# Attention gates ahead of the delta gates, query buffers taken by two blocks, one power for three row blocks

## The chip, the cores and the metric

The kernel runs on one core of a Trainium2 chip. The metric is device time in microseconds (us) of one execution. A core has a matrix engine (TensorE, PE in the rows; PEld is its loading of the stationary operand), a vector engine (VectorE, DVE), an engine for activation functions and copies (ScalarE, ACT), a general engine (GpSimd, POOL) and one that issues DMAs (SyncE, SP). Each takes its instructions in the order of the program and waits at an instruction until what it depends on is done. Results of TensorE land in PSUM, which is shared out here as two buffers for each of the names `tp`, `pj`, `sc` and `rc`.

## The reference

Two layers on 2048 prompt tokens and 8 samples of 16 tokens each, 1024 wide. Layer 0 mixes a sliding-window attention (branch A, 8 query heads) with a gated delta rule (branch B, 4 heads), each times its own SiLU gate; layer 1 is a pooling layer.

```python
def ab_layer(h, norm_g, w_in, ...):
    z = rms_norm(h, norm_g) @ w_in
    a_q, a_k, a_v, a_g, b_qkv, b_g, b_beta, b_alpha = split_cols(z, AB_WIDTHS)
    q = rms_norm(a_q.reshape(Bn, T, A_HEADS, A_HEAD_DIM), q_norm)
...
    o_a = o_a.reshape(Bn, T, A_WIDTH) * jax.nn.silu(a_g)
    c, new_hist = causal_conv(b_qkv, conv_hist, conv_w)
    bq, bk, bv = jnp.split(c, 3, axis=-1)
...
    o_b, s_new = gated_delta_rule(bq, bk, bv, beta, g, s0.astype(f32), chunk)
    o_b = rms_norm(o_b, o_norm).astype(h.dtype).reshape(Bn, T, B_WIDTH) * jax.nn.silu(b_g)
    y = h + jnp.concatenate([o_a, o_b], axis=-1) @ w_out
```

Inside the delta rule a unit lower triangular system is solved for each block of tokens (`triangular_solve`).

## The kernel before

**Groups and weights.** The tokens are worked in four groups of four blocks of 128 tokens; group 0 has the sample as a fifth block. Each group runs both layers. A matrix product is made of three products of split operands (a high and a low part each), so most products come in threes: L702 to L704 (weights move, 320 or 512 token columns), L1305 to L1307 (tokens stationary, 256 weight columns). `weight_plan` lists the weights' pieces in the order in which the code asks for them. In group 0 a piece is loaded, split by ScalarE (L471), VectorE and GpSimd (L475) and stored; later groups load the split form.

**Layer 0.** The heads are worked in two pairs. For a pair come keys, queries and values of branch B with their convolution (L885 to L901), the queries of branch A (`a_queries`), and in the background the inverse of the triangular system (`b_inverse`: 31 substitution steps on VectorE, L1019 and L1020; a transposing copy L1024; two stores to DRAM, L1026 and L1027; reloads in another shape, L1035 and L1037; products L1046 and on), the recurrence over the blocks (L1172 to L1220; for the sample L1233 to L1266, then L1272 and the scaling L1277), and the attention (`a_attend`, L1469 to L1500). Then come the gate columns of pair 0 (`gates_early(0)`) with `b_gated` (L1287 transposes the delta rule's result into `tp`, L1289 multiplies it) and `a_gated` (L1294, one VectorE product without a transpose), those of pair 1, and the output product (L735 to L737).

**The queries of branch A.** For each block the product lands in `pj`; ScalarE copies it to a buffer `zs` (L1400; the sample's L1397), the squares' sums go over ScalarE (L1319), VectorE (L1320, L1324) and a GpSimd power (L501), GpSimd multiplies (L1328, L1329). Deferred by `DEF`, `qcols` transposes the four heads' columns into `tp` (L1412); ScalarE (L1414) and VectorE (L1416) scale them into `qs` and so free `tp`.

**What sets the order.** Python code writes the program by a clock of its own: `tick` lets deferred steps (`defer`) and background jobs (`start`) go when their time has come. Large SBUF tiles are taken by hand from 11 big and 6 small buffers (`slot`, `drop`); if none is free, `slot` calls `progress()`, which writes the next deferred step or a job's next step at once. The names in the rows show the kind: `A` is a small buffer, `B` a big one.

**The start.** Blocks 0 and 1 are normalised by columns (`norm_input`), blocks 2 to 4 by `first_rows`: per block half the squares on ScalarE (L526) and half on VectorE (L528), a power on GpSimd (L501), the normalising product on VectorE (L545), then the transposes (L557), ScalarE's L560 and VectorE's L561.

## Time and profile before

| what | us |
|---|---|
| median of 3 runs | 1901.49 (1900.74 to 1903.12) |
| the profiled execution, its time | 1898.98 |
| its span in the trace | 1897.2 |
| TensorE busy in the span | 1824.5 |
| VectorE, ScalarE, GpSimd busy | 1196.4, 733.8, 498.8 |

The span runs from the first to the last instruction of the trace; the execution's own time is 1.8 us longer. Positions below are us from the span's start. Busy TensorE means that a product was under way; a row's idle time is what the engine stood before that instruction, with the instruction that released it.

### The profile page before, as it was taken

The page shows a single profiled execution, that of the slowest core. Times are in us where ns is not written, and L with a number is a line of the kernel's source. Part 1 is how long each engine was busy: PE and PEld are TensorE (multiplying, and loading weights), DVE is VectorE, ACT ScalarE, POOL GpSimd, SP SyncE. Part 2 cuts the span into 40 slices and gives each one's busy share as a digit, 9 for nine tenths or more (in the row PEclk, how much of TensorE's full clock was granted, in tenths as well). Part 3 has the DMA queues.
Part 4 walks back from the last instruction along what each step waited for, and adds up shares of the span by engine and source line. Part 5 has one row for each costly group of instructions (what it writes and reads, how often), then busy time and mean ns, then how long its engine had stood idle before and what let it go on. Part 6 is the DMA issues. An engine that isn't in the chain of part 4 may idle for free.

```text
span 1897.2 us, 30999 instructions
## 1 busy us (share of the span) xinstructions
PE 1824.5 (96%) x11434; PEld 1598.7 (84%) x11434; DVE 1196.4 (63%) x3184; ACT 733.8 (39%) x1883; POOL 498.8 (26%) x628
## 2 busy tenths in 40 slices
PE   6999989999999999999999999999999999999999
PEld 6888888889998888888888988888888988788887
DVE  6797967545664697764445597774345597764342
ACT  4465436323332474262222374261222474261210
POOL 5632451323332522310112413220012413220100
PEclk9998999999999999999999999999999999999999
DMA  7433362756668533435457533435467533435554
GB/s 277 144 133 125 120 226 76 250 195 208 229 234 293 214 119 105 167 118 189 171 204 282 208 115 108 166 130 188 161 217 278 204 117 118 148 134 189 182 189 186
DMA packets 94579, 337.52 MB, mean 178 GB/s; under 512 B 35884, under 2 KB 44332, under 8 KB 64988
## 3 DMA queue, kind: packets, MB, share of 16 engines
q1 hardware_dynamic: 94428, 335.54, 50.8%
q8 instruction: 90, 1.47, 0.3%
q14 instruction: 61, 0.50, 0.1%
HBM read 256.93 MB, written 78.58 MB: 177 GB/s over the span
## 4 chain that ended last, share of the span: by engine, by line
PE 74%; DVE 16%; POOL 3%; issue 3%; ACT 2%; DMA 2%; SPq 0%; DVEq 0%; POOLq 0%; ACTq 0%
PE pj L702 12%; PE pj L704 12%; PE pj L703 12%; PE pj L737 3%; PE pj L735 3%; PE pj L736 3%; PE rc L737 2%; PE rc L735 2%; PE rc L736 2%; DVE tm L1019 2%; DVE A L1020 2%; PE pj L1305 2%; PE pj L1306 2%; PE pj L1307 2%; PE tp L557 1%
## 5 line engine op out<-in xcount | busy, mean ns | idle before, releaser
L702 PE MATMUL pj<-XH,w 128*128 128x512 f32 (+3 forms) x1512 | 546.9, 362 | 5.5 <-ACT cb L876 3.4
L704 PE MATMUL pj<-XH,w 128*128 128x512 f32 (+3 forms) x1512 | 536.2, 355 | 0.0
L703 PE MATMUL pj<-XL,w 128*128 128x512 f32 (+3 forms) x1512 | 535.1, 354 | 0.0
L702 PEld LDWEIGHTS pj<-XH,w 128*128 128x128 f32 x1512 | 288.2, 191 | 33.7 <-ACT cb L876 3.7
L704 PEld LDWEIGHTS pj<-XH,w 128*128 128x128 f32 x1512 | 287.5, 190 | 29.3 <-issue 0.2
L703 PEld LDWEIGHTS pj<-XL,w 128*128 128x128 f32 x1512 | 288.0, 190 | 26.5 <-issue 0.2
L475 POOL TENSOR_TENSOR w<-wst,w 128x640 fp32r<-128x640 f32 (+2 forms) x60 | 105.2, 1754 | 179.0 <-ACT w L471 154.5
L1305 PE MATMUL pj<-w,XH 128*128 128x256 f32 (+1 forms) x368 | 106.8, 291 | 0.3 <-DVE VL L1351 0.3
L1307 PE MATMUL pj<-w,XL 128*128 128x256 f32 (+1 forms) x368 | 104.4, 284 | 0.0
L1306 PE MATMUL pj<-w,XH 128*128 128x256 f32 (+1 forms) x368 | 104.3, 283 | 0.0
L742 DVE TENSOR_TENSOR A<-pj,A 128x512 f32<-128x512 f32 x37 | 25.5, 689 | 101.4 <-PE pj L737 101.4
L737 PE MATMUL pj<-w,B 128*128 128x512 f32 x224 | 87.5, 391 | 0.0
L737 PE MATMUL rc<-w,B 128*128 128x512 f32 x212 | 82.6, 390 | 0.0
L471 ACT CAST w<-wst 128x1024 fp32r<-128x1024 f32 (+1 forms) x60 | 61.2, 1021 | 53.5 <-PE sc L737 42.0
L1723 DVE TENSOR_TENSOR B<-cb 128x526 f32<-128x526 f32 x32 | 24.1, 752 | 75.8 <-ACT cb L1775 75.7
L475 DVE TENSOR_TENSOR w<-wst,w 128x384 fp32r<-128x384 f32 (+2 forms) x60 | 48.1, 804 | 37.3 <-ACT w L471 37.1
L715 DVE SCALAR_TENSOR_TENSOR A<-A,pj 128x512 f32<-128x512 f32 (+1 forms) x33 | 21.1, 639 | 80.1 <-ACT A L714 79.8
L1305 PEld LDWEIGHTS pj<-w,XH 128*128 128x128 f32 x368 | 70.0, 190 | 1.7 <-DVE VL L1351 0.5
L1306 PEld LDWEIGHTS pj<-w,XH 128*128 128x128 f32 x368 | 70.1, 190 | 1.1 <-issue 0.5
L1307 PEld LDWEIGHTS pj<-w,XL 128*128 128x128 f32 x368 | 70.0, 190 | 0.0
L1019 DVE TENSOR_TENSOR tm<-A,A 40x31 f32<-40x31 f32 (+31 forms) x155 | 62.9, 406 | 6.8 <-DMA A<-Ld 4.4
L896 DVE SCALAR_TENSOR_TENSOR B<-cb,taps,B 128x512 f32<-128x512 f32 x78 | 57.8, 741 | 11.9 <-ACT B L885 11.2
(505 smaller groups left out, 4299.0 us busy)
## 6 DMA issues: line engine op xcount, KB each, us to landing
w<-wk SPq DMA_DIRECT2D x168, 1024.0 KB, 4.9
wk<-w SPq DMA_DIRECT2D x56, 1024.0 KB, 6.4
wst<-in_wts SPq DMA_DIRECT2D x56, 512.0 KB, 4.3
A<-in_x SPq DMA_DIRECT2D x22, 512.0 KB, 4.5
w<-wk SPq DMA_DIRECT2D x6, 1056.0 KB, 5.3
B<-in_x SPq DMA_DIRECT2D x12, 512.0 KB, 4.2
w<-wk SPq DMA_DIRECT2D x12, 512.0 KB, 3.3
out_y<-B SPq DMA_DIRECT2D x9, 512.0 KB, 2.6
```

Of the source, the lines that this page charges most:

```text
L471: S.copy(hi, st)
L475: eng.tensor_tensor(lo[:, a:b], st[:, a:b], f32(hi[:, a:b]), op=ALU.subtract)
L702: mm(pp[:, 0:w], wh[:, k, :], xh[:, k, t0:t1], start=(k == 0), stop=False)
L703: mm(pp[:, 0:w], wh[:, k, :], xl[:, k, t0:t1], start=False, stop=False)
L704: mm(pp[:, 0:w], wl[:, k, :], xh[:, k, t0:t1], start=False, stop=(k == KT - 1))
L735: mm(pp, oh[:, tk], wt[0][:, k, :], start=(kk == k == 0), stop=False)
L736: mm(pp, oh[:, tk], wt[1][:, k, :], start=False, stop=False)
L737: mm(pp, ol[:, tk], wt[0][:, k, :], start=False, stop=(kk == k == 1))
L1019: V.tensor_tensor(t3, bc(Lb[:, j + 1:32, j], w), bcm(Xb[:, j, 0:w], r), op=ALU.mult)
L1305: mm(pp[:, 0:N], xh[:, k, tk], wh[:, k % 4, :], start=(k == 0), stop=False)
L1306: mm(pp[:, 0:N], xh[:, k, tk], wl[:, k % 4, :], start=False, stop=False)
L1307: mm(pp[:, 0:N], xl[:, k, tk], wh[:, k % 4, :], start=False, stop=(k == KT - 1))
```

## The change

There are four edits.

1. Gates. In `gates_early(0)` the two attention gates come before the two delta gates, and `weight_plan` lists the weights so. For pair 1 the order stays.
2. `a_queries` no longer takes two `qs`, two `zs` and the sample's buffer at its start, but a `qs` and a `zs` at the first block of each two, and the sample's buffer at the sample block; a `zs` is dropped as soon as its second block's `qcols` is done.
3. `first_rows` makes all squares of its three blocks on ScalarE, then one power for the three, then the three normalising products, then the transposes.
4. At the start the third weight is split before the three blocks' norm is finished, not after.

```diff
+    def gates_a(pr):
+        for j in (2 * pr, 2 * pr + 1):
+            add("G", cols("in", np.concatenate([span(C_G + 256 * g + 64 * j, 64) for g in range(2)])))
+
+    gates_a(0)
     for pr in range(2):
         for h in (2 * pr, 2 * pr + 1):
             add("G", cols("in", span(C_BG + P * h, P)))
-        for j in (2 * pr, 2 * pr + 1):
-            add("G", cols("in", np.concatenate([span(C_G + 256 * g + 64 * j, 64) for g in range(2)])))
+    gates_a(1)
...
+        m = len(blocks)
+        ss = buf([P, 4, 2], "ss", 4)
+        for i, v in enumerate(xs):
+            for j in range(2):
+                junk = buf([P, 512], "t", NT)
+                S.activation(junk, v[:, 512 * j:512 * j + 512], AF.Square, accum_out=ss[:, i, j:j + 1])
+        rs = inv_rms(ss, m)
+        for i, v in enumerate(xs):
+            V.scalar_tensor_tensor(v, v, rs[:, i:i + 1], gain, op0=ALU.mult, op1=ALU.mult)
+        yield 0.0
         for b, v in zip(blocks, xs):
-            norm_rows(v, v, gain)
-            yield 0.0
             yield from norm_cols([v], b, *operand(0))
             drop(v)
...
     wpos[1] = 4
+    w_split(3)
     finish(norm_job2)
...
-            qs = [slot([P, 2, 4, P], F32R) for _ in range(2)]
-            zs = [slot([P, 2, 4, 2, 64]) for _ in range(2)]
+            qs, zs = [], []
             A = qh = None
-            if samp:
-
-                A = slot([P, 2, n])
-                qh = A[:, :, srow].rearrange("p c (j q) -> p c j q", q=64)
-                zs.append(A[:, 0, 0:256].rearrange("p (j g d) -> p j g d", j=2, d=64))
-            st["qh", jp] = (qs, qh, A)
             for b, pp in tok_major():
-                z = zs[b // 2][:, b % 2] if b < npb else zs[2]
+                if b == npb:
+
+                    A = slot([P, 2, n])
+                    qh = A[:, :, srow].rearrange("p c (j q) -> p c j q", q=64)
+                    zq = A[:, 0, 0:256].rearrange("p (j g d) -> p j g d", j=2, d=64)
+                if b < npb and b % 2 == 0:
+                    qs.append(slot([P, 2, 4, P], F32R))
+                    zs.append(slot([P, 2, 4, 2, 64]))
+                z = zs[b // 2][:, b % 2] if b < npb else zq
...
+                    if b % 2:
+                        drop(zs[b // 2])
 
                 defer(DEF, qcols)
 
+            st["qh", jp] = (qs, qh, A)
+
             def end():
-                drop(*zs[0:2])
                 st["A", jp] = start(a_attend(jp), 0.6)
...
         def gates_early(pr):
 
+            for j in range(2):
+                for pp, t0, t1 in proj_fm():
+                    gt = buf([P, 512], "t", NT)
+                    silu2(gt[:, 0:t1 - t0], pp)
+                    a_gated(pr, j, gt[:, 0:t1 - t0], t0, t1)
             for e in range(2):
...
                     if t1 == n:
                         b_gated(pr, e, gt)
-            for j in range(2):
-                for pp, t0, t1 in proj_fm():
-                    gt = buf([P, 512], "t", NT)
-                    silu2(gt[:, 0:t1 - t0], pp)
-                    a_gated(pr, j, gt[:, 0:t1 - t0], t0, t1)
```

The new lines move the line numbers: in the rows of the order below, those of the changed kernel are its own. L1019, L1020 and L1024 of before are L1032, L1033 and L1037; L1026 and L1027 are L1039 and L1040; L1266 is L1279; L1289 and L1294 are L1302 and L1307; L1319 is L1332; L1400, L1412, L1414 and L1416 are L1414, L1426, L1428 and L1430; L1185 and L1176 are L1198 and L1189; L501 is L505; L475 is L479; L715 is L728; L1287 is L1300; L1305 is L1318; L1328 and L1329 are L1341 and L1342.

**First place.** VectorE in group 1, where the last two query tiles of the second pair are scaled while the second pair's substitution runs. `tp` is the transposes' PSUM buffer, `t` the gate, `tm` the substitution's product. Before:

```order
L1416 SCALAR_TENSOR_TENSOR A_1557_8727<-tp_9012,gq_310,A_1557_8727 64x512
L1019 TENSOR_TENSOR tm_8855<-A_1513_8536,A_1514_8538 32x231
L1020 TENSOR_TENSOR A_1514_8538<-A_1514_8538,tm_8855 32x11x21
L715 SCALAR_TENSOR_TENSOR t_8958<-t_8958,pj_8961 128x512
L1019 TENSOR_TENSOR tm_8873<-A_1513_8536,A_1514_8538 32x220
L1289 SCALAR_TENSOR_TENSOR A_1267_7451<-tp_9027,on_h,t_8958 128x512
L1020 TENSOR_TENSOR A_1514_8538<-A_1514_8538,tm_8873 32x10x22
L1019 TENSOR_TENSOR tm_8882<-A_1513_8536,A_1514_8538 32x207
L1416 SCALAR_TENSOR_TENSOR A_1557_8727<-tp_9043,gq_310,A_1557_8727 64x512
```

After:

```order
L1430 SCALAR_TENSOR_TENSOR B_1578_8877<-tp_8999,gq_302,B_1578_8877 64x512
L1032 TENSOR_TENSOR tm_8800<-A_1507_8524,A_1508_8526 32x252
L728 SCALAR_TENSOR_TENSOR t_9012<-t_9012,pj_8948 128x512
L1033 TENSOR_TENSOR A_1508_8526<-A_1508_8526,tm_8800 32x14x18
L1307 SCALAR_TENSOR_TENSOR B_1285_7549<-B_1285_7549,t_9012 128x512
L1032 TENSOR_TENSOR tm_8812<-A_1507_8524,A_1508_8526 32x247
L1430 SCALAR_TENSOR_TENSOR B_1578_8877<-tp_9025,gq_302,B_1578_8877 64x512
```

The delta gate's product L1289, and with it TensorE's four transposes L1287 into `tp_9027`, is gone from between the two scalings; an attention gate's product L1307 stands there, which reads no `tp`. On TensorE the two batches of delta gate transposes are now among the attention's products, some 200 rows further on.

**Second place.** ScalarE in group 0, from the third block's copy of the second query pair on. The number behind a letter is the buffer, the last one counts the tiles. Before:

```order
L1400 COPY B6_588_3073<-pj_611_3196 128x4x64
L1400 COPY B6_588_3073<-pj_622_3262 128x4x64
L1319 ACTIVATE jka_608_3185<-B9_587_3072 128x256
L471 CAST w_639_3408<-wst_592_3082 128x1024
L1397 COPY B8_589_3074<-pj_627_3304 128x2x2x64
L900 ACTIVATE t_605_3165<-B5_406_2272 128x640
L1319 ACTIVATE jka_620_3254<-B6_588_3073 128x256
L471 CAST w_670_3568<-wst_638_3406 128x1024
L1140 ACTIVATE B5_406_2272<-tp_613_3212,b1_473_2537 128x128 x3
L1140 ACTIVATE B5_406_2272<-tp_614_3219,b1_473_2537 128x128 x2
L1319 ACTIVATE jka_625_3296<-B6_588_3073 128x256
L1414 ACTIVATE A5_576_3037<-tp_623_3275,gq8_310 128x512
```

After:

```order
L1428 ACTIVATE A5_578_3081<-tp_616_3262,gq8_302 128x512
L1198 ACTIVATE qs_644_3463<-rc_642_3457,eg_48_334 128x128
L1189 ACTIVATE kdt_645_3465<-rc_642_3457,eg_48_334 128x128
L1198 ACTIVATE qs_648_3473<-rc_646_3467,eg_48_334 128x128
L1428 ACTIVATE A5_578_3081<-tp_621_3304,gq8_302 128x512
L1189 ACTIVATE kdt_649_3475<-rc_646_3467,eg_48_334 128x128
L1414 COPY A2_611_3238<-pj_602_3181 128x4x64
L1414 COPY A2_611_3238<-pj_615_3249 128x4x64
L1332 ACTIVATE jka_613_3241<-A2_611_3238 128x256
```

and SyncE's queue there after:

```order
L1694 DMA out_s_bconv<-cvs_327 128x288
L1279 DMA out_s_bs<-A2_556_2958 128x1024
L1246 DMA B1_759_4004<-in_state_s 128x1024
L1040 DMA Xd_607_3211<-A4_488_2629 40x1024
L1039 DMA Xd_607_3211<-A2_606_3209 40x1024
L1050 DMA A3_609_3216<-Xd_607_3211 32x10x32 x2
L1048 DMA B9_608_3214<-Xd_607_3211 32x10x32 x3
```

Before, the third and fourth block's copies L1400 stand early and write a big buffer, B6; the first two query tiles' scalings L1414 come after them. After, the copies (L1414 now) stand behind the first two tiles' scalings (L1428 now) and write buffer A2, which was the sample's state (`A2_556`) and then the transposed inverse (`A2_606`) that L1039 stores.

**Third place.** GpSimd at the start, from the first power of `first_rows` on (`rs` is its result, `rsa` that of the attention keys' norm, `w` a weight's low part). Before:

```order
L501 TENSOR_TENSOR rs_239<-ms_236,first 128x1
L501 TENSOR_TENSOR rsa_380<-ssa_375,first 128x2
L1328 TENSOR_TENSOR B_56_345<-B_56_345,rsa_380 128x2x64
L501 TENSOR_TENSOR rs_264<-ms_261,first 128x1
L1329 TENSOR_TENSOR B_56_345<-B_56_345,rsa_380 128x2x64
L501 TENSOR_TENSOR rsa_418<-ssa_413,first 128x2
L1328 TENSOR_TENSOR B_56_345<-B_56_345,rsa_418 128x2x64
L501 TENSOR_TENSOR rs_289<-ms_286,first 128x1
L1329 TENSOR_TENSOR B_56_345<-B_56_345,rsa_418 128x2x64
L475 TENSOR_TENSOR w_432<-wst_225,w_432 128x640
```

After:

```order
L505 TENSOR_TENSOR rsa_373<-ssa_368,first 128x2
L1341 TENSOR_TENSOR B_51_337<-B_51_337,rsa_373 128x2x64
L1342 TENSOR_TENSOR B_51_337<-B_51_337,rsa_373 128x2x64
L505 TENSOR_TENSOR rs_251<-ms_248,first 128x3
L479 TENSOR_TENSOR w_231<-wst_225,w_231 128x640
L505 TENSOR_TENSOR rsa_411<-ssa_406,first 128x2
```

Three powers of one column became one of three columns, behind the first key block's products, and a weight's L475 (L479 now) stands right behind it.

## Rows read from the trace of the kernel before

**Rows 1.** Here is the page's first part: busy us of each engine, its share of the span, and its instructions.

```profile
PE 1824.5 (96%) x11434; PEld 1598.7 (84%) x11434; DVE 1196.4 (63%) x3184; ACT 733.8 (39%) x1883; POOL 498.8 (26%) x628
```

**Rows 2.** Here is who kept TensorE waiting, over the whole span. Columns: engine, tile and line that waited, what it waited for, us in total, how often, the longest in us.

```profile
PE tp L1412 <- POOL B L1329: 6.0, 3, 3.4
PE tp L1412 <- DVE A L1416: 5.6, 3, 1.9
...
PE tp L557 <- DVE XL L561: 3.8, 1, 3.8
...
PE tp L1287 <- DVE A L1416: 2.0, 3, 0.7
```

**Rows 3.** Here is the timeline of group 1 where the queries' tiles of the second pair meet the first gate columns, TensorE and then VectorE. Columns: start in us, length in us, engine, line, operation, tiles, shape, count; in brackets the idle time before and what ended it.

```profile
779.03 0.66 PE L1287 MATMUL tp<-first,A 128*128 128x128 f32 x4 [0.63 <-DVE A L1416]
...
783.00 0.63 PE L1412 MATMUL tp<-first,B 128*128 128x128 f32 x4 [1.91 <-DVE A L1416]
...
778.22 0.76 DVE L1416 SCALAR_TENSOR_TENSOR A<-tp,gq,A 64x512 fp32r<-64x512 f32 x1
...
782.10 0.76 DVE L1416 SCALAR_TENSOR_TENSOR A<-tp,gq,A 64x512 fp32r<-64x512 f32 x1
```

**Rows 4.** Here is busy time by stretch for the same place in group 1 and for the 65 us behind it. Columns: the stretch, its length, then busy us and instructions of TensorE, its weight loads, VectorE, ScalarE and GpSimd, granted clock (1.00 is 2.4 GHz), share and rate of DMA.

```profile
775.00:785.00 10.00, 7.46 (x38) 5.67 (x38) 9.54 (x21) 1.98 (x3) 3.28 (x5) 1.00 0.47 180
785.00:850.00 65.00, 64.57 (x468) 55.07 (x467) 41.86 (x149) 33.56 (x98) 9.61 (x12) 1.00 0.42 134
```

**Rows 5.** Here is the timeline of TensorE in group 0, from the last step of the delta rule on the sample to the first transposes of the second query pair.

```profile
239.69 1.88 PE L1261 MATMUL sc<-t,kdt 128*128 128x512 f32 x4
...
249.47 0.77 PE L1138 MATMUL tp<-first,B 128*128 128x128 f32 x5
...
252.17 0.66 PE L1412 MATMUL tp<-first,B 128*128 128x128 f32 x4 [1.12 <-POOL B L1329]
256.20 0.68 PE L1412 MATMUL tp<-first,B 128*128 128x128 f32 x4 [3.37 <-POOL B L1329]
```

**Rows 6.** Here is the same stretch on VectorE (two steps L1264 of the sample's state that have a step of the substitution between them, one step L1019 of the substitution by itself, the transposing copy L1024), then ScalarE's scaling L1414 of a query tile, GpSimd's powers L501 and products L1277, L1328 and L1329, and the first reload L1035 in SyncE's DMA queue (SPq; the length is that of the issue).

```profile
228.28 0.33 DVE L1264 SCALAR_TENSOR_TENSOR A<-A,eg,sc 128x128 f32<-128x128 f32 x1
...
228.87 0.33 DVE L1264 SCALAR_TENSOR_TENSOR A<-A,eg,sc 128x128 f32<-128x128 f32 x1
...
254.19 0.21 DVE L1019 TENSOR_TENSOR tm<-A,A 40x60 f32<-40x60 f32 x1
...
258.97 1.21 DVE L1024 COPY A<-A 40x1024 f32<-40x1024 f32 x1
...
256.91 0.69 ACT L1414 ACTIVATE A<-tp,gq 128x512 fp32r<-128x512 f32 x1 [3.36 <-PE tp L1412]
...
243.06 2.15 POOL L501 TENSOR_TENSOR ro<-so,first 128x5 f32<-128x5 f32 x1 [2.57 <-DVE so L1272]
245.28 2.47 POOL L1277 TENSOR_TENSOR B<-B,ro 128x640 f32<-128x640 f32 x1
...
253.76 1.00 POOL L501 TENSOR_TENSOR rsa<-ssa,first 128x4 f32<-128x4 f32 x1
254.84 0.61 POOL L1328 TENSOR_TENSOR B<-B,rsa 128x256 f32<-128x256 f32 x1
255.53 0.61 POOL L1329 TENSOR_TENSOR B<-B,rsa 128x256 f32<-128x256 f32 x1
...
263.69 0.32 SPq L1035 DMA_DIRECT2D B<-Xd  x1
```

**Rows 7.** Here is busy time by stretch around that place and to the end of group 0's first layer; the columns as in rows 4.

```profile
247.00:268.00 21.00, 14.93 (x91) 13.75 (x90) 15.26 (x31) 9.62 (x22) 17.15 (x19) 0.84 0.58 195
256.70:263.50 6.80, 5.24 (x23) 4.80 (x22) 4.80 (x8) 2.52 (x6) 6.49 (x8) 0.50 0.98 398
...
290.00:440.00 150.00, 143.01 (x903) 124.67 (x903) 88.25 (x235) 65.89 (x167) 40.23 (x30) 0.99 0.55 185
```

**Rows 8.** Here is the pace of TensorE's big products in the stretch of group 0: two starts of L702 (320 columns) and two of L1305 (256 columns), each three products apart.

```profile
216.43 0.31 PE L702 MATMUL pj<-XH,w 128*128 128x320 f32 x1
...
216.87 0.31 PE L702 MATMUL pj<-XH,w 128*128 128x320 f32 x1
...
242.12 0.28 PE L1305 MATMUL pj<-w,XH 128*128 128x256 f32 x1
...
242.47 0.28 PE L1305 MATMUL pj<-w,XH 128*128 128x256 f32 x1
```

**Rows 9.** Here is the start of group 0: the last three row blocks' norm. VectorE's half squares L528 and the normalising L545, ScalarE's half squares L526, GpSimd's powers L501, TensorE's transposes L557.

```profile
21.17 0.68 DVE L528 SCALAR_TENSOR_TENSOR t<-A 128x512 f32<-128x512 f32 x1
...
25.24 2.62 DVE L545 SCALAR_TENSOR_TENSOR A<-A,rs,B 128x1024 f32<-128x1024 f32 x2
...
21.65 0.63 ACT L526 ACTIVATE t<-A 128x512 f32<-128x512 f32 x1
...
28.87 0.54 POOL L501 TENSOR_TENSOR rs<-ms,first 128x1 f32<-128x1 f32 x1
...
22.57 0.39 PE L702 MATMUL pj<-XH,w 128*128 128x256 f32 x1 [1.02 <-DVE VL L1351]
...
26.58 1.09 PE L557 MATMUL tp<-first,A 128*128 128x128 f32 x8 [0.89 <-DVE A L545]
31.52 1.11 PE L557 MATMUL tp<-first,A 128*128 128x128 f32 x4 [3.84 <-DVE XL L561]
```

More of the change, by code (lines that the diff above doesn't have):

```diff
@@ L1401, in a_queries, with qcols @@
                     head_norm(z[:, :, 0, :], 4, z[:, :, 1, :], qms[:, 4 * jp:4 * jp + 4])
-                def qcols(z=z, b=b):
+                def qcols(z=z, b=b, qh=qh):
                     pt = psum("tp")
```

## The prediction

> **What bounds the kernel now.** I read the page's busy times first: TensorE is busy 1824.5 us of the span of 1897.2, 96%, and the next engine, VectorE, 63% [rows 1]. So an edit gains only where TensorE stands still, and loses wherever it makes TensorE stand still. Next I read the waits of TensorE over the span [rows 2]. The change can reach four of them. The queries' transposes L1412 wait 6.0 us in three waits for GpSimd's L1329 and 5.6 us in three for VectorE's L1416; the delta gates' transposes L1287 wait 2.0 us in three for L1416; a transpose of the first norm waits 3.8 us once. Then I looked at each place in the timeline.
>
> In group 1 [rows 3] the third query tile's L1416 ends at 778.98 behind a row of substitution steps, and L1287, which wants its buffer of the two tp buffers, starts at 779.03 after 0.63 us of idleness. The L1416 after that ends at 782.86, and the fourth L1412 starts at 783.00 after 1.91 us. The stretch 775 to 785 holds 7.46 us of TensorE work in 10 us, at the full clock, and the 65 us behind it are idle for 0.43 us [rows 4]. Groups 2 and 3 have the same waits once each (the "3" in rows 2). In group 0 the 6.0 us lie in one place, 251 to 262 [rows 5].
>
> **Part 1, the gate order in groups 1 to 3.** After the change no L1287 stands between the query tiles (the first order fence): the fourth tile takes the buffer of the second, not of the third, and the four transposes of each delta gate come far behind, inside the attention units. Both waits go: 5.6 + 2.0 = 7.6 us [rows 2]. What is late next? The eight L1287 per group meet L1483's transposes in the same two buffers, and fewer gate products are left between the attention's steps. That place of before has 0.43 us of idleness in 65 us [rows 4], so its chains are covered today, and I cannot read how much cover is to spare. Bounds: nothing, or in each group a wait as long as the mean of the six removed ones, 7.6 / 6 = 1.3, so 3.8 in all. I take 1.0 in all, nearer to nothing, since 0.43 of 65 is the nearest row. Gain 6.6, between 7.6 and 3.8.
>
> **Part 2, the start.** The three last blocks' squares go to ScalarE alone: VectorE loses three L528 of 0.68, ScalarE gets three more halves of 0.63 [rows 9]. The first L702 waits 1.02 for VectorE there [rows 9], and with L528 out of VectorE's way most of that wait goes. Against it, one power now serves all three blocks and waits for the last square; the first transposes (26.58) therefore come later by up to one half square and a normalising, 0.63 + 1.31 = 1.9. The third block's transposes (31.52, after 3.84 idle) come earlier, because its power no longer stands at 28.87 behind other GpSimd work; the three normalisings run back to back. Gains and losses are of one size; bounds: 1.0 gained at the first L702 and 0.5 (a power, 0.54) at the third block, or 1.9 lost less the 1.0. I take 0.5 gained. Splitting weight 3 before the norm only moves work that ScalarE, VectorE and GpSimd do while TensorE waits anyway: nothing.
>
> **Part 3, the second query pair of group 0.** This edit decides. The queries' tiles are now taken two blocks at a time, in the middle of the projection, when the small buffers have been used up by the delta rule and its inverse. The second order fence shows what the third block's copy L1414 (L1400 before) writes: A2_611, the buffer that was A2_606, the transposed inverse, which VectorE's copy L1037 (L1024 before) fills and the store L1039 (L1026 before) reads. So that copy now waits until the whole 31-step substitution has ended and its store has landed. Behind it on ScalarE stand the fourth block's copy and the norm squares; on TensorE the sample block's products wait for the bank of this copy, and everything is behind them, for TensorE goes in order. Walked out from rows:
>
> - TensorE. L1261 starts at 239.69 before [rows 5]. In the new order 21 more products L1305 stand ahead of it, at 0.35 / 3 = 0.117 [rows 8] 2.5 us, and the five L1138 with five short products, which before took from 249.47 to 251.05 (252.17 less the wait of 1.12), 1.6 us [rows 5]. That is 243.8 at the earliest; I add 0.7, one VectorE product like L1416, because the last convolution rows now stand ahead of its operand: 244.5. The pair ends at 246.4 (1.88).
> - VectorE. The eight state steps L1264 alternate with substitution steps, a pair each 0.59 (228.28 to 228.87) [rows 6]: 4.7 us from 245.4, when the first of the two products ends. With four short rows at about 0.25 the power's input so is ready at 251.1.
> - GpSimd. Two powers, 1.00 for the tile and 2.15 for so, L1328 0.61, L1277 2.47, L1329 0.61 [rows 6]: 6.8, so the second tile's transposes start at 257.9 (256.20 before). With the short power twice it is 5.7.
> - Back: transposes 0.66, L1414 0.69 [rows 5, 6], L1416 0.76 [rows 3], eight substitution steps at 0.21 to 0.3, say 2.0, and L1024 1.21 [rows 6]: 263.2. From that copy's end (260.18) to the first reload, which waits for its store, 3.51 passed [rows 6]: 266.7. Then the copy runs, some 0.4, and TensorE starts again at about 267.1.
>
> So between 246.4 and 267.1 TensorE would have 1.5 us of work (two tiles and a short product) and be idle 19.2. Before, that stretch is idle 6.07 (21.00 less 14.93 [rows 7], of which 1.12 and 3.37 are in rows 5): 13.1 lost. TensorE ran at 1.2 GHz from 256.7 to 263.5 with 5.24 busy [rows 7], which cost before 2.6; after two longer stops I expect one stretch like it that holds half as much work, 1.7 lost: 0.9 back. By 246.4 the new order is behind by some 0.7 (twenty L1305, 2.3, less the 1.6 brought forward). Sum 12.9. Later the inverse's products have 24 fillers in place of the many of today; I put 1.0 for a stall there. And work that is behind fills today's holes: from 290 to 440 TensorE idles 6.99 [rows 7]; I take a third, 2.4. **Loss 11.5**. Bounds: 12.9 less 1.1 (short power), 0.7 and all 7.0 of the holes, 4.1; or 12.9 plus 1.0, 2.0 for stalls and nothing regained, 15.9.
>
> One rule bears on the store's 3.51. The Trainium skill, SBUF — State Buffer, section "The DMA setup-cost knee", gives each transfer a roughly fixed 2 us. By that estimate the loss would be 10.0 and the sum 1.5 us smaller; the trace has 3.51 for this same store, so that stands.
>
> **Sum.** -6.6 - 0.5 + 11.5 = +4.4 us on the profiled execution's 1898.98, 1903.4. That execution lies 2.5 under the median of the runs, 1901.49; on the median the forecast is **1905.9**. 0.2%, 3.8 us, is about what a measurement of this kernel can tell from no change.
>
> **Rivals.**
> - *The late work fills the holes.* Part 3 as walked, but short powers and most of the 6.99 idle us regained: loss near 5, net -2, about 1899.5. For it: TensorE is the only bound later on. Against: those holes are waits of short chains, which fillers reach only if they stand there in the order.
> - *The buffer was free in time.* If the inverse ends long before the third block's copy (VectorE has five fewer rows in front of L1024: three L1320, two L475), part 3 costs nothing and parts 1 and 2 stay: -7.1, 1894.4; it decides if L1024's store lands before about 247. Against it: the state steps alone keep VectorE to 250.
> - *The attention units lose their cover.* Slower, from another place: in groups 1 to 3 each delta gate's L1287 waits as L1412 does today, 1.91 twice a group, 11.5 in all; with part 3 at 5 that is -7.6 - 0.5 + 5 + 11.5 = +8.4, 1909.9. It decides as soon as the fillers that moved (eight transposes a group) covered a chain of that length. The 0.43 speaks against.
>
> **How the numbers follow.** Forecast (part 3 loses 9 to 16, net +1 to +10): 0.45, of which 0.14 stays within 3.8 us. Holes filled: 0.23. Buffer free: 0.19. Attention units: 0.13. The range leaves out half of the free-buffer case and the upper ends: 1895.5 to 1912. Faster by over 0.2% is the free-buffer case and a quarter of the holes, 0.19 + 0.06 = 0.25. Within 0.2%: the rest of the holes and the forecast's low part, 0.17 + 0.14 = 0.31. Slower: 0.31 + 0.13 = 0.44.
>
> **What would show it.** In the profile after: no L1412 or L1287 waiting for L1416 in groups 1 to 3 (part 1); the first L702 near 21.6 and the third block's transposes before 31.5 (part 2); a wait of TensorE's L1318 (L1305 before) for the copy L1414 of 7 us or more near 260, with that copy behind the store of the inverse, and the clock at 1.2 GHz there (part 3). I am wrong if that wait is under 3 us, or if group 0 ends no later than today.

## The result, and the profile after

The changed kernel takes 1907.71 us (median of 7 runs, 1903.24 to 1911.75), the kernel before on the same chip 1900.74 (7 runs, 1898.54 to 1904.66). The ratio is 1.0032, interval 1.0021 to 1.0042: slower by 6.1 us. The forecast was slower by 4.4. Here is the first part of the changed kernel's page:

```profile
span 1902.9 us, 31020 instructions
PE 1825.7 (96%) x11434; PEld 1602.0 (84%) x11434; DVE 1197.2 (63%) x3174; ACT 734.9 (39%) x1889; POOL 487.7 (26%) x626
```

TensorE has as many products as in [rows 1] and is busy for 1.2 us more; the span is 5.7 us longer. So 4.5 us of the change are in TensorE's waits. Here they are for the changed kernel, as in [rows 2]:

```profile
PE tp L1426 <- POOL B L1342: 8.8, 1, 8.8
PE pj L1318 <- ACT A L1414: 8.3, 2, 7.7
...
PE sc L1059 <- DMA A<-Xd: 4.3, 2, 2.4
...
PE tp L561 <- DVE A L623: 2.2, 1, 2.2
...
PE tp L1426 <- POOL A L1342: 1.9, 1, 1.9
PE pj L715 <- ACT w L475: 1.7, 1, 1.7
```

What part 1 was to remove is gone: no line names L1430 (L1416 before) any more, 7.6 us less. New ones stand there: two long waits in group 0, one at a query tile in group 1 (1.9), and 4.3 us in two waits at L1059, the first product of the inverse, for its reload. For a stall at the inverse's products the prediction has 1.0 us in group 0, and nothing in groups 1 to 3.

**Group 0.** TensorE's timeline, which answers [rows 5]:

```profile
241.16 2.05 PE L1274 MATMUL sc<-t,kdt 128*128 128x512 f32 x4 [0.25 <-DVE t L1272]
243.05 0.60 PE L1426 MATMUL tp<-first,B 128*128 128x128 f32 x4
...
252.63 1.12 PE L1426 MATMUL tp<-first,B 128*128 128x128 f32 x4 [8.75 <-POOL B L1342]
261.47 0.58 PE L1318 MATMUL pj<-w,XH 128*128 128x256 f32 x1 [7.73 <-ACT A L1414]
```

And who kept it waiting, in [rows 6]'s engines: the last state step, the short row `so` and the transposing copy on VectorE, the powers and the second tile's product on GpSimd, the copy of the third block on ScalarE, the inverse's store on SyncE's queue:

```profile
246.28 0.33 DVE L1277 SCALAR_TENSOR_TENSOR A<-A,eg,sc 128x128 f32<-128x128 f32 x1
...
247.49 0.15 DVE L1285 SCALAR_TENSOR_TENSOR so<-so,ssq 128x5 f32<-128x5 f32 x1
...
257.37 1.05 DVE L1037 COPY A<-A 40x1024 f32<-40x1024 f32 x1
...
247.64 1.13 POOL L505 TENSOR_TENSOR rsa<-ssa,first 128x4 f32<-128x4 f32 x1 [5.54 <-DVE so L1285]
...
250.62 1.33 POOL L1290 TENSOR_TENSOR B<-B,ro 128x640 f32<-128x640 f32 x1
251.91 0.66 POOL L1342 TENSOR_TENSOR B<-B,rsa 128x256 f32<-128x256 f32 x1
...
261.05 0.65 ACT L1414 COPY A<-pj 128x256 f32<-128x256 f32 x2 [6.32 <-DMA Xd<-A]
...
258.45 0.29 SPq L1039 DMA_DIRECT2D Xd<-A  x1
```

It is the chain that was walked out, link by link. The substitution ends, the copy L1037 ends at 258.42, its store goes out at 258.45, and ScalarE's copy, which writes the store's buffer, starts at 261.05 "<-DMA". TensorE resumes 0.42 later. The stops are 8.75 + 7.73 = 16.5 us.

Two stretches of the changed kernel show what it cost besides; the columns are those of [rows 4]:

```profile
246.30:266.80 20.50, 6.44 (x41) 5.82 (x42) 11.57 (x32) 4.29 (x10) 9.05 (x11) 0.50 0.29 81
295.40:445.40 150.00, 143.19 (x922) 126.31 (x921) 85.58 (x204) 63.23 (x152) 42.26 (x30) 1.00 0.58 196
```

TensorE ran at 1.2 GHz all through the first, with 6.44 us of work in it, so 3.2 us went to the clock. The second is the later part of the layer, as long as the stretch 290 to 440 of [rows 7], which had 143.01 us of work: 143.19 is 0.2 more. The late work filled no holes.

**The start**, against [rows 9]:

```profile
26.62 1.09 PE L561 MATMUL tp<-first,A 128*128 128x128 f32 x8 [2.16 <-DVE A L623]
29.39 0.58 PE L715 MATMUL pj<-XH,w 128*128 128x256 f32 x1 [1.67 <-ACT w L475]
29.98 1.05 PE L561 MATMUL tp<-first,A 128*128 128x128 f32 x4
```

The first L715 waits for nothing now, and the 3.84 us are gone that stood before the transposes at 31.52. The prediction calls those the third block's, but they are the second's: each block has eight transposes, and the third's start at 35.04 before and 33.95 after. Against the gain, 2.16 stand before the first transposes (0.89 before), and 1.67 where TensorE wants the next weight from ScalarE's L475.

**Group 2.** The inverse of its second pair, in the kernel before, then in the changed kernel (SyncE's second store, TensorE's first product):

```profile
1220.58 0.32 SPq L1026 DMA_DIRECT2D Xd<-A  x1
1228.34 0.69 PE L1046 MATMUL sc<-A,B 32*32 32x32 f32 x16
```

```profile
1223.61 0.32 SPq L1039 DMA_DIRECT2D Xd<-A  x1
1230.45 0.66 PE L1059 MATMUL sc<-A,B 32*32 32x32 f32 x16 [1.94 <-DMA A<-Xd]
```

Before, the product came 7.76 after the store and did not wait. Now TensorE is there 1.94 early and starts 6.84 after the store. In group 3 the same wait is 2.40 us, and TensorE then runs at half clock:

```profile
1652.70:1659.40 6.70, 6.37 (x28) 4.72 (x28) 0.00 (x0) 0.37 (x1) 0.00 (x0) 0.50 0.44 157
```

That took another 3.2 us (6.37 of work at half speed), in this trace: in e5, which takes the tiles in the same way there, the stretch at 1.2 GHz is 3.4 us long (1652.1 to 1655.5), all of it work, so 1.7. Waits and clock in groups 1 to 3, 1.91 + 1.94 + 2.40 + 3.2 = 9.5 us, stand in this trace against the 7.6 removed.

### The profile page after: what moved, and what is told of

Its sections match the earlier page's. It is cut to its first block, busy times and chain, and to the rows that moved or that the text cites. A ratio compares the mean times of both kernels' runs of the same rounds, so it can differ in the third digit from the quotient of the medians.

```text
span 1902.9 us, 31020 instructions
## 1 busy us (share of the span) xinstructions
PE 1825.7 (96%) x11434; PEld 1602.0 (84%) x11434; DVE 1197.2 (63%) x3174; ACT 734.9 (39%) x1889; POOL 487.7 (26%) x626
## 4 chain that ended last, share of the span: by engine, by line
PE 74%; DVE 15%; ACT 4%; issue 3%; POOL 2%; DMA 1%; SPq 0%; DVEq 0%; ACTq 0%; POOLq 0%
PE pj L717 12%; PE pj L716 12%; PE pj L715 12%; PE pj L748 3%; PE pj L750 3%; PE pj L749 3%; PE rc L750 2%; PE rc L748 2%; PE rc L749 2%; DVE tm L1032 2%; PE pj L1319 2%; PE pj L1318 2%; PE pj L1320 2%; DVE A L1033 1%; DVE B L909 1%
## 5 line engine op out<-in xcount | busy, mean ns | idle before, releaser
L715 PE MATMUL pj<-XH,w 128*128 128x512 f32 (+3 forms) x1512 | 544.6, 360 | 3.2 <-ACT w L475 1.7
L715 PEld LDWEIGHTS pj<-XH,w 128*128 128x128 f32 x1512 | 286.6, 190 | 33.1 <-ACT w L475 1.9
L479 POOL TENSOR_TENSOR w<-wst,w 128x640 fp32r<-128x640 f32 (+2 forms) x60 | 105.0, 1751 | 173.6 <-ACT w L475 169.9
L1318 PE MATMUL pj<-w,XH 128*128 128x256 f32 (+1 forms) x368 | 107.9, 293 | 8.7 <-ACT A L1414 8.3
L1319 PE MATMUL pj<-w,XH 128*128 128x256 f32 (+1 forms) x368 | 106.2, 289 | 0.3 <-DVE w L479 0.3
L755 DVE TENSOR_TENSOR B<-pj,B 128x512 f32<-128x512 f32 x48 | 33.2, 691 | 103.8 <-PE pj L750 103.8
L909 DVE SCALAR_TENSOR_TENSOR B<-cb,taps,B 128x512 f32<-128x512 f32 x90 | 69.8, 776 | 20.2 <-ACT B L898 19.5
L475 ACT CAST w<-wst 128x1024 fp32r<-128x1024 f32 (+1 forms) x60 | 61.3, 1022 | 51.5 <-PE sc L750 41.9
L1318 PEld LDWEIGHTS pj<-w,XH 128*128 128x128 f32 x368 | 71.6, 195 | 10.1 <-ACT A L1414 8.9
L750 PE MATMUL pj<-w,B 128*128 128x512 f32 x200 | 78.2, 391 | 0.0
L479 DVE TENSOR_TENSOR w<-wst,w 128x384 fp32r<-128x384 f32 (+2 forms) x60 | 49.6, 827 | 42.3 <-ACT w L475 42.1
L750 PE MATMUL rc<-w,B 128*128 128x512 f32 x188 | 73.2, 390 | 0.0
L1319 PEld LDWEIGHTS pj<-w,XH 128*128 128x128 f32 x368 | 71.6, 194 | 1.1 <-DVE w L479 0.5
L728 DVE SCALAR_TENSOR_TENSOR A<-A,pj 128x512 f32<-128x512 f32 (+1 forms) x33 | 21.1, 639 | 75.8 <-ACT A L727 75.6
L505 POOL TENSOR_TENSOR rsa<-ssa,first 128x4 f32<-128x4 f32 (+1 forms) x51 | 49.4, 969 | 62.0 <-DVE ssa L1335 27.6
```

The source lines that it names most:

```text
L475: S.copy(hi, st)
L479: eng.tensor_tensor(lo[:, a:b], st[:, a:b], f32(hi[:, a:b]), op=ALU.subtract)
L715: mm(pp[:, 0:w], wh[:, k, :], xh[:, k, t0:t1], start=(k == 0), stop=False)
L750: mm(pp, ol[:, tk], wt[0][:, k, :], start=False, stop=(kk == k == 1))
L909: V.scalar_tensor_tensor(dst[:, 0:Tp], cb[:, j:j + Tp], taps[:, m, j:j + 1], dst[:, 0:Tp], op0=ALU.mult, op1=ALU.add)
L1318: mm(pp[:, 0:N], xh[:, k, tk], wh[:, k % 4, :], start=(k == 0), stop=False)
```

## The experiments

All times are beside runs of the kernel before on the same chip; us are the ratio less 1, times 1901.

| label | what | median | ratio (interval) | us |
|---|---|---|---|---|
| after | the change | 1907.71 | 1.0032 (1.0021 to 1.0042) | +6.1 |
| e1_gates | before, gates alone | 1896.06 | 0.9975 (0.9965 to 0.9984) | -4.8 |
| e2_queries | before, queries alone | 1906.52 | 1.0034 (1.0021 to 1.0048) | +6.5 |
| e3_start | before, start alone | 1900.28 | 0.9996 (0.9987 to 1.0005) | -0.8 |
| e4_gates_start | after without the queries | 1892.23 | 0.9961 (0.9949 to 0.9974) | -7.4 |
| e10_first | e4, queries new in the first pair of group 0 | 1885.69 | 0.9922 (0.9909 to 0.9935) | -14.8 |
| e7_group0 | e10, and in the second pair | 1902.04 | 1.0003 (0.9995 to 1.0012) | +0.6 |
| e12_push | e7, buffers and order mended | 1888.55 | 0.9933 (0.9919 to 0.9947) | -12.7 |
| e5_buffer | after, third block in another buffer | 1898.23 | 0.9988 (0.9978 to 0.9997) | -2.3 |
| e9_fresh | e5, and fresh buffers passed over | 1900.51 | 1.0007 (0.9997 to 1.0018) | +1.3 |
| e6_xtw | after, inverse's products later | 1913.45 | 1.0061 (1.0048 to 1.0073) | +11.6 |
| e8_xtw | e4, inverse's products later | 1901.21 | 1.0003 (0.9994 to 1.0012) | +0.6 |
| e11_queue | e4, three reloads by GpSimd | 1903.99 | 1.0022 (1.0009 to 1.0034) | +4.2 |

**e1 to e4: the parts alone.** The edits are those of the diff ahead.

e1: 

> Part 1 alone: the kernel before with the attention gates in front of the delta gates, nothing else. My theory after reading the changed kernel's trace: the removed waits (2.5 us in each of groups 1 to 3, 7.6 in all) had slack under them, because the inverse's first product L1046 waits for a chain on VectorE and the DMA that does not get earlier with them; so new waits of about 2 us a group stand at that product, and the whole gains 0.5 to 2.5 us (1899 against 1900.7 median). Rival A, the waits were on the path as predicted: 5.5 to 7.6 us gained, near 1894.5. Rival B, the edit loses by itself in group 3 (a wait there and a drop of the clock): 1 to 3 us lost, no gain.

e2: 

> Part 3 alone: the kernel before with the queries' tiles taken by two blocks, nothing else. Theory: the third block's copy of group 0's second pair waits for the buffer of the inverse; TensorE waits 7 us or more there, and group 0's first layer ends 9 to 11 us later; groups 1 to 3 keep their waits of 2.5 us each. Whole: 8 to 12 us lost, 1909 to 1913. Rival A, the loss is only what the changed kernel's group 0 shows at its end, 5 us: 1905 to 1907. Rival B, the loss needs the new start or the new gates: under 3 us lost.

e3: 

> Part 2 alone: the kernel before with one power for the last three row blocks of the first norm, and the splitting of weight 3 in front of it. By the prediction 0.5 us gained (bounds 1.5 gained to 0.9 lost). By the changed kernel's trace, which is 5 us ahead at 200 us: 0.9 us from shorter waits in the first 60 us, and the rest from waits further on and from the clock, which may be chance: if they come with this edit, 4 to 6 us gained at 200 us and 3 to 5 at the end, 1896 to 1898; if they are chance or come from the queries' order, 0.5 to 1.5 gained, 1899 to 1900.

e4: 

> The changed kernel without the queries' edit, so parts 1 and 2 together. Theory, additive: part 1's 0.5 to 2.5 gained and part 2's 0.5 to 4, so 1895 to 1899, and against the changed kernel 9 to 11 us faster. Rival, the parts hang together (the gates only gain with the new query buffers): the same time as the kernel before within 2 us.

The gates alone gain 4.8 us, between my new theory and the prediction. Their waits, in e1:

```profile
PE sc L1050 <- DMA A<-Xd: 3.4, 3, 1.6
```

Of the 7.6 us 3.4 come back at the inverse's first product (here L1050), once in each of the three groups. The chain under it did not move: counted from the transposes L557 that end the group before (904.02 before, 904.69 in e1), the second store in group 2 goes out at 316.56 before (1220.58) and at 316.82 in e1 (1221.51); TensorE comes to the product at 322.2 in place of 324.3. The queries alone lose 6.5, as rival A said and less than I thought; their trace has the same two stops in group 0 (8.76 and 7.74). The start gains 0.8, within its interval of nothing. Gates and start together gain 7.4, additive within the intervals and more than I expected. So the queries' edit on top of them costs 7.4 + 6.1 = 13.5, more than the 6.5 alone: the edits do not add up, and why is open.

**e5: another buffer for the third block** of group 0's second pair.

```diff
-                    zs.append(slot([P, 2, 4, 2, 64]))
-                z = zs[b // 2][:, b % 2] if b < npb else zq
+                    zs.append(slot([P, BIG if samp and jp and b else SMALL]))
+                z = zs[b // 2][:, 512 * (b % 2):512 * (b % 2) + 512].rearrange(
+                    "p (i e d) -> p i e d", i=4, d=64) if b < npb else zq
```

> The changed kernel, but in group 0 the second pair's third and fourth block take a big buffer that has long been free, in place of the one that held the transposed inverse; the rest as changed. Theory (part 3 of the prediction): TensorE's wait of 7.7 us for the copy behind the inverse's store goes, the wait of 8.8 us for GpSimd's product stays or is filled by the sample block's products that no longer stand behind the copy; group 0's first layer ends 5 to 9 us earlier than in the changed kernel, groups 1 to 3 as there: 1899 to 1903. Rival: VectorE's state steps and substitution set the end there whatever the buffer, so the wait only moves to the inverse's first product: under 2 us gained, 1906 to 1908.

8.4 us came back. On ScalarE the third block's copy (L1415 here) now runs before the inverse has ended, and TensorE, which has the sample block's products to do, waits for GpSimd alone, 5.51 us here and 0.96 once more:

```profile
241.21 0.37 ACT L1415 COPY B<-pj 128x256 f32<-128x256 f32 x1 [1.88 <-PE pj L1320]
...
256.21 1.11 PE L1427 MATMUL tp<-first,B 128*128 128x128 f32 x4 [5.51 <-POOL B L1342]
```

The wait of 7.7 was the buffer's, and 8.8 became 5.5 because the products behind the copy fill part of it. In this trace group 0's first layer ends 4.45 us earlier than in the changed kernel (434.44 for 438.89); the traced run, 1902.42, lies 4.2 over the median of e5's runs.

**e7 and e10: where the queries' edit costs.** A flag takes the tiles at the pair's start, as before, except in group 0 (e7), or in its first pair alone (e10).

```diff
+            lazy = samp                  # e10: samp and jp == 0
+            if not lazy:
+                qs += [slot([P, 2, 4, P], F32R) for _ in range(2)]
+                zs += [slot([P, 2, 4, 2, 64]) for _ in range(2)]
```

e7: 

> The changed kernel with the queries' tiles taken by two blocks in group 0 alone; groups 1 to 3 take them as before. Theory (the queries' edit costs in groups 1 to 3 too, because four buffers taken at once push the pending work of other jobs ahead, and taken by two they don't): groups 1 to 3 gain 4 to 5 us over the kernel before as with the gates alone, group 0 ends as in the changed kernel, so 1900 to 1904, 4 to 7 faster than the changed kernel. Rival: the loss of the gates' gain comes from where group 0 ends or from chance of the clock: 1906 to 1908.

e10: 

> Gates and start, with the queries' tiles taken by two blocks for group 0's first pair alone. In the traces of the queries' edit alone and of the changed kernel, TensorE is 3 to 4 us ahead between the first pair and 200 us (the stall of 2.95 us at 93 us is gone). Theory: this lead is the edit's and stays: 1888 to 1890. Rival, by the sums of the medians (the edit's loss in group 0 is 9.8 us, and the buffer alone explains 9.5): the lead is used up before the layer ends: 1891.5 to 1893.

Three steps, from e4 to the changed kernel: the first pair of group 0 gains 7.4 (e10), its second pair loses 15.4 (e7), groups 1 to 3 lose 5.5 (after). e7's time is in the range of its theory; that buffers taken at once push other jobs' work ahead in groups 1 to 3, which the theory gives as the reason, it does not show. e10's lead stays to the end; it is 14.8 us faster than the kernel before, more than I expected. Its TensorE stops in group 0's second pair are short:

```profile
246.89 0.77 PE L1151 MATMUL tp<-first,B 128*128 128x128 f32 x5 [1.75 <-DVE B L914]
...
251.14 1.03 PE L1435 MATMUL tp<-first,B 128*128 128x128 f32 x4 [2.01 <-POOL B L1342]
```

Here is where the first pair's 7.4 us come from: the stretch from 60 to 445 in e4 and two stops of e4's TensorE there, then the same stretch and one stop in e10 (columns as in [rows 4] and [rows 3]):

```profile
60.00:445.00 385.00, 356.14 (x2649) 326.21 (x2650) 273.90 (x815) 175.69 (x472) 142.15 (x137) 0.97 0.48 161
96.02 0.58 PE L1482 MATMUL sc<-KH,A 128*128 128x256 f32 x1 [2.95 <-DVE mx L1486]
...
145.00 0.41 PE L715 MATMUL pj<-XH,w 128*128 128x320 f32 x1 [3.31 <-ACT cb L889]
```

```profile
60.00:445.00 385.00, 362.96 (x2708) 332.42 (x2707) 284.15 (x831) 181.19 (x481) 138.33 (x143) 0.99 0.50 166
148.29 0.39 PE L1526 MATMUL sc<-pT,VH 128*128 128x256 f32 x1 [3.18 <-DVE mx L1501]
```

TensorE is idle for 28.9 us of the stretch in e4 and for 22.0 in e10. Both of e4's stops are gone; the one at L1526 was 1.97 in e4. In the second pair e4 waits three times for GpSimd, 6.0 us in all (the kernel before has the same [rows 2]), where e10 has the two stops above. What in the order ends each of these waits was not tested.

**e12: what the second pair's loss is made of.** When the old code took the pair's tiles in group 0, no buffer was free five times, and `slot` wrote five steps of the sample's delta rule ahead of the pair. Taken late, the tiles force nothing, and these steps stand behind 21 products. e12 takes the tiles late, but from big buffers, and writes the five steps ahead:

```diff
+            if samp and jp:
+                for _ in range(5):
+                    progress()
...
-                    zs.append(slot([P, 2, 4, 2, 64]))
+                    zs.append(slot([P, BIG if jp else SMALL]))
```

> The changed kernel with the queries' tiles taken by two blocks in group 0 alone, but in group 0's second pair from big buffers that are long free, and with the five steps of other jobs' work written ahead of the pair that the old code forced there because no buffer was free (the sample's delta rule, its state and its power). So both pairs still take their tiles late, and only what followed from it is put back. Theory (the second pair's loss of 16.3 us, 1902.0 less 1885.7, is two things: 9.5 for the copy behind the inverse's store, and the rest because the delta rule's steps stand behind 21 products): both go, and the time is that of the kernel whose second pair takes its tiles in the old way, 1885 to 1888. Rival: taking them late costs by itself, so only the buffer's 9.5 comes back: 1891 to 1894.

13.3 of the 15.4 come back, and the interval overlaps that of e10; the time is 0.6 us above the range of the theory and far from the rival's. So taking a tile late costs by itself nothing that can be told from these runs; what cost was the buffer, 8.4 by e5, and the order, some 5 (13.3 less 8.4). No run mends the order alone: its 5 is a difference of four medians, known to within some 4 us.

**e6 and e8: the inverse's products later.** One number: `XTW` 5.0 to 7.0 in the changed kernel, to 6.5 in e4.

e6: 

> The changed kernel with one number of the order changed: the inverse's first product stands 7.0 us (of the planner's own time) behind the issue of its reloads, in place of 5.0. Theory (the waits of 1.9 and 2.4 us at that product in groups 2 and 3 are TensorE arriving too early at a chain that VectorE and the DMA set, with other products left that could go first): both waits go, with them the half clock of group 3 (3.2 us): 3 to 7 us gained, 1901 to 1905. Rival: the products that would go first are needed later on, and the state steps behind the inverse come later in their turn: no gain within 1.5 us, since the wait only moves to another product.

e8: 

> Gates and start alone (no queries' edit), with the inverse's first product 6.5 us behind its reloads in place of 5.0. Theory: its waits of 1.1, 1.5 and 1.2 us in groups 1 to 3 go, 2 to 4 us gained over gates and start alone (1892.2): 1888.5 to 1890.5. Rival: later products wait in their turn: 1891.5 to 1894.

My theory fell in both: 5.5 and 8.0 us lost. In e6 the wait in group 2 moved to the attention's transposes L1500, which now wait for ScalarE:

```profile
PE tp L1500 <- ACT B L1464: 7.3, 2, 3.9
...
1227.72 1.53 PE L1500 MATMUL tp<-first,B 128*128 128x128 f32 x5 [3.38 <-ACT B L1464]
```

In e8 the same transposes (L1496 there) wait 7.7 us. So the products that I thought free to go first had been the cover of the attention units.

**e11: three of the seven reloads issued by GpSimd.**

```diff
-                    Q.dma_start(XA[o:o + 32, 0:nh, 32 * (b % 2):32 * (b % 2) + 32],
+                    G.dma_start(XA[o:o + 32, 0:nh, 32 * (b % 2):32 * (b % 2) + 32],
```

> Gates and start, with the three reloads of the inverse's untransposed half issued from GpSimd in place of SyncE's queue. Theory (the waits of 1.1 to 1.5 us at the inverse's first product in groups 1 to 3 are set by the chain copy, stores, seven reloads one behind another): the last reload is issued 1.3 us earlier, the waits go, 2 to 4 us gained over gates and start alone: 1888 to 1890. Rival: a reload issued from GpSimd lands later than one from SyncE, or stands behind GpSimd's own work: no gain or up to 4 us lost, 1892 to 1896.

11.6 us lost against e4. Around group 2's inverse:

```profile
A<-Xd SPq DMA_DIRECT2D x4, 32.0 KB, 3.8
A<-Xd POOLq DMA_DIRECT2D x3, 32.0 KB, 4.1
...
1226.90 0.67 PE L1059 MATMUL sc<-A,B 32*32 32x32 f32 x16 [2.04 <-DMA A<-Xd]
```

GpSimd's reloads land after 4.1 us, SyncE's after 3.8. The store went out at 1220.18 and the last reload was issued by 1224.33, 4.15 after it; in e4 that took 5.36 (1220.64 to 1226.00). But the product starts 6.72 after the store, in e4 6.87. So of 1.2 us in the issuing 0.15 reach the product: here the issuing was not the limit, the landing is. Why the whole is so much slower is open: the edit shifts other instructions too.

**e9: are fresh buffers the cause in groups 1 to 3 as well?**

```diff
-            if size <= SMALL and free_small:
+            if size <= SMALL and free_small and (
+                    len(free_big) < 3 or now[0] - freed.get(free_small[0], -99.0) > 6):
```

> The changed kernel with the big buffer of the earlier run in group 0, and one rule more for taking buffers everywhere: a small buffer that was dropped less than 6 us (of the planner's time) ago is passed over while at least three big ones are free. Theory (the queries' edit costs in groups 1 to 3 for the same reason as in group 0: the tiles' early drop keeps the small list from being empty, so the inverse's reload buffer becomes the one whose store is still in flight; store to first reload took 3.4 us in the changed kernel's group 1 and 2.0 with the old queries): that distance is 2.0 again, and 4 to 6 us more are gained than with the big buffer alone (1898.2): 1891 to 1895. Rival: in groups 1 to 3 the loss hangs on something else in taking the tiles late (GpSimd's order), so 1897 to 1900.

The rule did what it was to do. Stores and first reloads of group 1's first inverse, in the changed kernel and in e9:

```profile
721.76 0.33 SPq L1039 DMA_DIRECT2D Xd<-A  x1
...
725.12 0.38 SPq L1048 DMA_DIRECT2D A<-Xd  x1
```

```profile
721.18 0.33 SPq L1042 DMA_DIRECT2D Xd<-B  x1
...
723.19 0.81 SPq L1051 DMA_DIRECT2D B<-Xd  x2
```

3.36 us became 2.01. The time did not follow: 1900.51 is above the ranges of theory and rival, and 3.6 us more than e5 by the ratios. In group 0 the rule itself made new stops (4.35 and 4.72 at query tiles), and the first layer ends at 439.69, in e5 at 434.44. For groups 1 to 3 here is the stretch from the first weight product of group 1 (L715, in e9 L718) to the first of group 3's second layer, in the changed kernel, e5, e9, e7 and e4; columns as in [rows 4]:

```profile
636.49:1752.49 1116.00, 1099.77 (x6683) 940.26 (x6682) 710.42 (x1971) 444.38 (x1177) 241.95 (x356) 1.00 0.48 167
632.03:1749.90 1117.87, 1101.06 (x6683) 942.56 (x6681) 709.82 (x1971) 443.90 (x1177) 242.40 (x356) 1.00 0.48 167
635.60:1748.24 1112.64, 1097.94 (x6682) 939.61 (x6681) 710.18 (x1971) 445.64 (x1177) 235.14 (x356) 1.00 0.48 168
637.77:1749.57 1111.80, 1098.38 (x6682) 940.25 (x6681) 708.49 (x1971) 445.73 (x1177) 244.07 (x356) 1.00 0.48 168
630.38:1745.42 1115.04, 1100.30 (x6683) 941.15 (x6681) 708.03 (x1971) 445.77 (x1177) 244.47 (x356) 1.00 0.48 167
```

e9 takes 3.4 us less than the changed kernel and 5.2 less than e5, as the theory said, and waits 2.9 us at the inverse's first product in place of 4.3. But e7 and e4 have the same order on TensorE here and stand 3.2 apart (e1, also with this order, takes 1110.5), so single traces can't decide about 3 to 5 us. The theory is neither shown nor ruled out.

That the edit costs 5.5 us in groups 1 to 3 is measured; by which wait is not settled. The wait of 1.91 us for GpSimd at a query tile of group 1 stands in all traces with the tiles taken late there (the changed kernel, e2, e5; 2.24 in e9) and not in e1, e4, e7, e10 and e12; but those wait 1.1 to 2.1 us at the inverse's first product of group 1 instead.

## Why the prediction was right or wrong

**The sum is near (+4.4 against +6.1), and the mechanism of its main term is shown, but that it is so near is in part luck: the main term came out 3.9 larger, and two effects that were left out, -7.4 and +5.5, nearly cancel.**

- *Part 1, predicted -6.6, alone -4.8.* The mechanism holds: all six waits went. The step that failed is "What is late next?". I looked for it at the delta gates, bounded it by 3.8 and took 1.0; it came as 3.4 us at the inverse's first product, some 20 us further on. The waits removed were partly slack of a chain (31 substitution steps on VectorE, copy, stores, reloads, in all 6.3 to 6.9 us in group 2 from the second store to the product) which does not get earlier when TensorE does. The attention units kept their cover until e6 and e8 took it from them.
- *Part 2, predicted -0.5, alone -0.8 (interval 2.5 gained to 1.0 lost).* Both signs stand as drawn: the first L715 waits for nothing and starts before 21.6, and the transposes that stood at 31.52 start at 29.98 (the second block's, as said above). What I missed is a cover: the split of the next weight ends on ScalarE at 29.3 in both kernels (28.23 + 1.06, 28.28 + 1.06); the wait of 3.84 hid it, and now 1.67 shows.
- *Part 3, group 0's second pair, predicted +11.5.* The mechanism is shown by e5 and e12. Link by link: GpSimd 4.9 (247.64 to 252.57) where I had 6.8 (5.7 with the short power); from the copy's end to the freed buffer 2.6, where I had 3.51. That was the distance to the store's first reload, and this too is shorter now (L1048 at 261.01, 2.59 after the copy's end). The DMA was 0.98 busy there before [rows 7] and 0.29 in the first of the two stretches above; whether that is the reason no run tests. Further: stops 16.5 in place of 19.2; clock 3.2 lost where I had 1.7; holes regained 0.2 of 2.4. L1274 started 3.3 us earlier than walked (241.16 for 244.5) and TensorE resumed 5.6 earlier (261.47 for 267.1), so the layer ended only 5.4 later (438.89 for 433.53); the early start fits the first pair's gain below. Against the same kernel with the old second pair the loss is 15.4, near the upper bound of 15.9.
- *Left out.* The first pair of group 0 was not costed and gains 7.4: the stops of 2.95 and 3.31 us before the second pair go (e10), and the waits in the second pair are shorter. In groups 1 to 3 the queries' edit was taken as free; it costs 5.5 by the medians, so that of the gates' 4.8 nothing is left in the changed kernel; by which wait is open.

By the numbers of the table: -7.4 for parts 1 and 2, -7.4 for group 0's first pair, +15.4 for its second, +5.5 for groups 1 to 3, sum +6.1. The forecast's own split was -7.1 for parts 1 and 2 and +11.5 for the second pair.

**Rivals.** "The buffer was free in time" is ruled out by the copy at 261.05. "The late work fills the holes" is too: 0.2 us. "The attention units lose their cover" named a cost in the right groups, but the waits stand elsewhere; it is what e6 and e8 show.

**The rule on the DMA's fixed 2 us.** The store that the copy waits for took 2.6 us from its issue (258.45 to 261.05); the Trainium skill, SBUF — State Buffer, section "The DMA setup-cost knee", has roughly 2, and the trace lies between that and my 3.51, nearer to the page. Elsewhere it varies: in group 1 a store's first reload goes out 3.36 us after it in the changed kernel and 2.01 in e9.

## What to carry to other kernels

A wait removed from the busiest engine is worth only what the next operand's own chain allows: before counting it as gain, follow the engine to the next operand that another engine's chain delivers, and see how long before its use it is ready. Where buffers are handed out from a list, changing when a tile is taken changes whose buffer it gets and what the allocation pushed ahead; look at the last reader of the buffer, above all a store in flight, in every group and not only where the edit hurts most. And split a change that gains in one place and loses in another: here its best part alone is worth 14.8 us, and the whole costs 6.1.

## What the runs showed of the hardware

TensorE's clock is not the same from run to run in the same work. Here are 10.5 us of group 0 that begin 1.05 us before L702 resumes from a stop, in the kernel before and in e1 (L706 there), whose orders are the same up to there; columns as in [rows 4]:

```profile
144.00:154.50 10.50, 8.42 (x33) 8.02 (x34) 6.27 (x19) 5.28 (x17) 4.57 (x3) 0.51 0.74 215
```

```profile
145.77:156.27 10.50, 7.46 (x40) 6.46 (x40) 6.28 (x19) 5.10 (x17) 4.57 (x3) 0.84 0.68 209
```

The granted clock is 0.51 in one and 0.84 in the other, round stops of nearly the same length (3.42 and 3.29 us). At the end of group 0's first layer the two stand 2.0 us apart (its transposes start at 433.53 and 435.50), though nothing in the edit speaks for a loss there. So a difference of that size is to be read from medians, not from single traces. And in the changed kernel two long stops have TensorE at 1.2 GHz for 20.5 us, three times as long as the stretch of [rows 7], and the clock still costs only 3.2, because little work was there.
